# Half of the value projection in 512-column matmuls ahead of all scores, and later key projections begun before the scores of the pair ahead

## The chip, the cores and the metric

The kernel runs on one core of one Trainium2 chip. The core has a matrix engine (TensorE, PE in the profile; its weight loads are PEld), a vector engine (VectorE, DVE), a scalar engine (ScalarE, ACT), GpSimd (POOL), and SyncE (SP), whose queue issues all the DMAs of this kernel. Each engine works through its own instructions in order and waits for the others at semaphores. The metric is the device time of one execution in microseconds (us), as the median of a few runs. A profile is one more execution with the hardware profiler on; its span reaches from the first to the last instruction.

## The reference, cut to what matters

A decoder trunk for one sequence of 512 tokens with 1024 channels, all float32: a pooling layer with an MLP, then an attention layer with an MLP. The change lies in the attention layer. Keys and values come from one projection of the normed residual stream, queries from another, for 16 heads of 64 channels:

```
kv = jnp.matmul(rms_norm(x, kv_norm_g), w_kv).reshape(B, S, 2, N_HEADS, HEAD_DIM)
k = kv[:, :, 0].transpose(0, 2, 1, 3)
v = kv[:, :, 1].transpose(0, 2, 1, 3)
...
q = jnp.matmul(h, w_q[j]).reshape(B, S, N_HEADS, HEAD_DIM).transpose(0, 2, 1, 3)
o = stick_breaking_attention(q, k, v)
m = jnp.matmul(o.transpose(0, 2, 1, 3).reshape(B, S, HD), w_o[j])
```

Stick-breaking attention takes, for each query, the sigmoid of each score times the product of (1 - sigmoid) over all keys between that key and the query, and weighs the values with it; it is strictly causal. The kernel forms the products with a scan along the keys.

## The kernel before, in words

**Precision and matmuls.** Every float32 operand is split into a high part (a copy rounded to the matmul's type, on ScalarE) and a low part (the rest, a subtraction on VectorE). A product of two split operands is three matmuls: high x high, high x low, low x high (`mm3`, and `up_block` with the roles of the operands exchanged). A matmul streams up to 512 columns against a stationary 128x128 block into one bank of PSUM, of which there are eight; all of them go round under one tag, `ps`.

**Attention, by steps.** The 16 heads are eight pairs of two. The attention layer is written as a list of steps, `ATT_ORDER`, and TensorE runs them in exactly this order; the order of the other engines' instructions is left to the scheduler. A word of the list is a letter, an index and sometimes digits:

- `V` u, tiles: value projection for group u (four heads, 256 columns) and the named token tiles of 128. It is 24 matmuls of 256 columns per tile (8 channel blocks x 3), the normed tokens stationary and the weights moving, into half a bank; then ScalarE copies the high part and VectorE subtracts for the low part. Two weight tiles per group.
- `N` t: transposition of the normed token tile t of the layer's input (8 PE transposes, two copies, two subtractions). Tiles 2 and 3 are left over from the MLP before.
- `K` i: begins the key projection of pair i (`start`). `P` i: the rest of that key projection and the query projection of pair i (`project`, `queries_keys`), 24 matmuls of 512 columns each where nothing was begun, with the weights stationary and the tokens moving; then the splits `kh`, `kl`, `qh`, `ql`.
- `S` i: the scores of pair i (24 matmuls into six banks), and behind them the weights (`weights`): on ScalarE sigmoids of both signs (`against` writes `u`, `for_` writes `w`), on VectorE, head by head, a scan over 1280 entries (`scan`, tile `e`) and a product (`weigh`, tile `w`).
- `T` i: transposition of the weights of pair i, ten 128x128 transposes for its first head, then ten for its second, with copies `ah` and subtractions `al`. The first head's transposes wait for its `weigh`, the second head's for the other `weigh`.
- `A` i: products with the values (two banks), and the output pair `ohl` (`out_low`, `out`, `split`).
- `O` u, tiles: output projection of pairs 2u and 2u+1, added up in `y`. `E`: the end of the layer, in an order written out for all engines (`END_ORDER`).

**Before the change**, the list spreads the values over the layer: `V0` for tiles 0 and 1 covers the wait for `N2`, half of `K0` (its first 256 token columns) the wait for `N3`; `V1` stands in single tiles around the transposes of pairs 0 and 1.

**Weights.** All weights of the layer but two are scaled and split during the first MLP and put back into DRAM (`split_apart`, dictionary `kept`); they come back as two 512 KB DMAs each into one of four buffers (`w` three times, `wx` once), each DMA waiting for the last matmul on what the buffer held. `want` puts weights into a queue in the order of the list, `fill` and `make` issue the loads. The first two output weights (`("o", 0)`, `("o", 1)`) are not kept: they arrive raw and are split on ScalarE (line 170) and VectorE (line 172) during the attention layer. `behind` holds the last instructions of each engine, behind which later splits of weights may be issued.

Of the kernel before, what the change touches and what calls it, by code (L numbers as in the profile page):

```python
# [27 lines left out]
HD = 64  # L28
# [4 lines left out]
TS = [slice(t * P, (t + 1) * P) for t in range(T)]  # L33
NS = [slice(0, 512), slice(512, 1024)]
# [23 lines left out]

ATT_ORDER = [
    (w[0], int(w[1]), [int(c) for c in w[2:]])  # L60
    for w in """V001 N2 K0 N3 V02 P0 V03 S0 P1 V10 T0 V11 S1 A0 P2 T1 V12 A1 V13 S2 P3 T2 O00123 A2 S3 P4 V201 T3 S4
    A3 P5 V22 T4 V23 S5 A4 P6 V30 T5 V31 S6 A5 V323 P7 T6 E1""".split()
]


# [36 lines left out]
C_MIX_PRE0, C_KV, C_MIX_PRE1, C_MLP_PRE1 = range(4)  # L102
# [3 lines left out]
def trunk(ctx, tc, x, consts, grow, pw, wup, wdn, wq, wk, wv, wo, out):  # L106
    nc = tc.nc
# [22 lines left out]
    ident, gc = eye[:, :P], eye[:, P:]  # L130
# [23 lines left out]
    behind, latest = {}, {}  # L154
# [20 lines left out]
    def gains(lo, n):  # L175


        def scaled(raw):
            for k in range(n):
                c = raw[:, k * D // n : (k + 1) * D // n]  # L180
                nc.scalar.mul(c, c, gc[:, lo + k : lo + k + 1])  # L181
# [23 lines left out]
    apart, kept, going = [], {}, []  # L205
# [31 lines left out]
    def make():  # L237
        k, src, scaled = queue.pop(0)
        if k in kept:
            made[k] = place(k)  # L240
            for n, t in enumerate(made[k]):
                latest["sp"] = nc.sync.dma_start(t.bitcast(F32), kept[k][n])
            return
        made[k] = weight(src, place(k), scaled, dn_raw.pop(k, None))

    def fill(n=1):
        if gate[0]:
            behind.update(latest)
        for _ in range(n):
            if queue and len(made) < ahead and (queue[0][0][0] != "dn" or dn_pool[0]):  # L250
                make()

    def get(key):
        while key not in made:
            make()
        return made.pop(key)

    for l in range(2):
        if l == 1:
            n = len(queue)  # L260
            for what, i, part in ATT_ORDER:
                if what == "V" and 0 in part:
                    for h in range(2):
                        want(("v", i, h), wv[i, h], gains(C_KV * KC + 4 * h, 4))
                elif what == "P":
                    want(("k", i), wk[i], gains(C_KV * KC, KC))
                    want(("q", i), wq[i], gains(C_MIX_PRE1 * KC, KC))
                elif what == "O" and 0 in part or what == "E":
                    for c in range(2 * i, 2 * i + 2 if what == "O" else PAIRS):
                        want(("o", c), wo[c])  # L270
            apart.extend(x for x in queue[n:] if x[0] not in [("o", c) for c in range(2)])

            queue[n - GRP : n + GRP] = queue[n : n + GRP] + queue[n - GRP : n]
        for j in range(NJ):
            want(("up", l, j), wup[l, j])
        for j in range(NJ - GRP, NJ):
            want(("dn", l, j), wdn[l, j])
# [21 lines left out]
    def mm3(dst, ah, al, bh, bl, start, stop):  # L299
        nc.tensor.matmul(dst, ah, bh, start=start, stop=False)  # L300
# [193 lines left out]
    def y_tiles():  # L494
        return [work.tile([P, D], F32, tag=f"y{t}", name=name(f"y{t}")) for t in range(T)]
# [204 lines left out]
        fill(ahead)  # L700
        finish(l, squares[1:], w, y, lambda t, y: update(t, y, gpost))

    def up_block(pu, w, cols, last=False):
# [6 lines left out]
        for k in range(KC):  # L710
            nc.tensor.matmul(pu[:, cols], wh[:, k, :], xnh[:, k, cols], start=k == 0, stop=False)  # L711
            nc.tensor.matmul(pu[:, cols], wh[:, k, :], xnl[:, k, cols], start=False, stop=False)  # L712
            if not last:
                low(k)
        if last:
            for k in range(KC):
                low(k)


    with tc.tile_pool(name="mix0", bufs=1, reuse_waits="tile") as mp:  # L720
# [12 lines left out]
        at = P + 4 * KC  # L733
# [145 lines left out]
    with tc.tile_pool(name="att", bufs=1, reuse_waits="tile") as ap:  # L879
        att_pool[0] = ap  # L880

        def values(u, part):
            if u not in vs:
                w = [get(("v", u, h)) for h in range(2)]
                vs[u] = w, ap.tile([P, T, 4, 2, HD], F32R, tag="v", bufs=2, name=name("v"))
            w, v = vs[u]
            for s in part:
                need(s)
# [7 lines left out]
                pv4 = pv[:, :256].rearrange("p (h d) -> p h d", h=4)  # L896
                nc.scalar.copy(v[:, s, :, 0, :], pv4)
                nc.vector.tensor_tensor(
                    out=v[:, s, :, 1, :], in0=pv4, in1=v[:, s, :, 0, :].bitcast(F32), op=ALU.subtract
                )  # L900

        started = {}

        def start(key):

            need(0, 1)
            started[key] = ps(), get(key)
            up_block(*started[key], slice(0, S // 2))

        def project(key):  # L910
            need(*range(T))
            if key in started:
                pq, w = started.pop(key)
                up_block(pq, w, slice(S // 2, S))
            else:
                pq = ps()
                up_block(pq, get(key), slice(0, S))
            return pq
# [176 lines left out]
        vs, os, wos, y = {}, {}, {}, y_tiles()  # L1095
# [6 lines left out]
        def end():  # L1102

            p, last = PAIRS - 2, PAIRS - 1
            heads[last] = [Head(qk[last], last, a) for a in range(2)]
            w = {c: get(("o", c)) for c in range(2, 6)}
# [104 lines left out]
            with tc.manual_schedule(engines={on.PE, on.Activation, on.DVE, on.Pool, on.SP}):  # L1211
                for step, which in END_ORDER:
                    steps[step](*which)

        def until(key):
            while key not in made:
                make()
# [2 lines left out]

        def step(what, i, part):
            nonlocal gpost1
            if what == "V":
# [86 lines left out]
```

## Time and profile before

| what | value |
|---|---|
| time, median of 3 runs | 949.31 us (949.29 to 949.32) |
| time of the profiled execution | 949.25 us |
| its span | 947.4 us |
| TensorE busy | 938.1 us, 99% of the span, 4822 matmuls |
| VectorE, ScalarE, GpSimd busy | 73%, 59%, 4% |
| granted TensorE clock | 0.998 |
| DMA | 156.17 MB, mean 165 GB/s |

The profiled execution takes 1.85 us more than its span. Lines of a group view read: line of the kernel, engine, operation, output<-input, shape, count, busy time, mean duration. A line of the timeline reads: start (us), duration (us), engine, line, operation, tiles, shape, count, and in brackets how long the engine was idle before it and what ended that. A line of the table by windows reads: window, its length, then for each engine the busy time and the instructions that touch the window (those that reach across its edges included), the granted clock, the busy share of the DMA engines and GB/s. The attention layer lies at 368 to 592 us of the span.

### The profile page before, as it was taken

Reading aid. Unit: us, or ns where it says so; the run is one execution under the profiler, and the core shown is the slowest. Engines: PE = TensorE matmul, PEld = TensorE weight load, DVE = VectorE, ACT = ScalarE, POOL = GpSimd, SP = SyncE. Lnnn points to the kernel's source line nnn. Section 1 sums busy time; section 2 is a strip of 40 time slices with the busy share of each in tenths; the row PEclk is TensorE's granted clock in tenths of the full one; section 3 lists DMA queues with packets and bytes.
Section 4 is the critical chain, followed back from the end, with each engine's and each line's share of the span. In section 5 each row is a group of like instructions: output and inputs, shape, how many; then the busy total and the mean of one; then the engine's idle time right before and its main releaser. Section 6 shows DMA issues by size and latency. Waiting matters only on the chain.

```text
span 947.4 us, 12570 instructions
## 1 busy us (share of the span) xinstructions
PE 938.1 (99%) x4822; PEld 796.4 (84%) x4822; DVE 696.0 (73%) x797; ACT 559.1 (59%) x983; POOL 41.2 (4%) x83
## 2 busy tenths in 40 slices
PE   9999999999999999999999999999999999999996
PEld 7998888888888889888888988898888888888885
DVE  5875798988979876366466678874696966958756
ACT  6667979888775547345554444865545444444532
POOL 2300000000000004000000001200000000000002
PEclk9999999999999999999999999999999999999999
DMA  8254969789697760522425261442514233133102
GB/s 310 95 180 145 344 218 346 291 285 353 217 330 282 271 203 2 194 87 93 175 97 178 104 253 45 140 150 80 187 45 137 85 133 111 45 134 111 39 6 90
DMA packets 43263, 156.17 MB, mean 165 GB/s; under 512 B 4289, under 2 KB 4673, under 8 KB 43202
## 3 DMA queue, kind: packets, MB, share of 16 engines
q1 hardware_dynamic: 43202, 155.36, 46.4%
q8 instruction: 38, 0.62, 0.3%
q14 instruction: 23, 0.19, 0.1%
HBM read 121.79 MB, written 33.55 MB: 164 GB/s over the span
## 4 chain that ended last, share of the span: by engine, by line
PE 94%; DVE 1%; ACT 1%; POOL 1%; DMA 1%; issue 1%; SPq 0%; POOLq 0%; DVEq 0%; ACTq 0%
PE ps L589 28%; PE ps L711 15%; PE ps L708 15%; PE ps L712 15%; PE ps L300 4%; PE ps L302 4%; PE ps L301 4%; PE ps L1023 2%; PE ps L1048 2%; PE ps L1006 2%; PE ps L829 1%; PE ps L395 1%; ACT xn L285 1%; DMA band<-in_consts 1%; PE ps L801 1%; POOL stat L296 1%
## 5 line engine op out<-in xcount | busy, mean ns | idle before, releaser
L589 PE MATMUL ps<-w,a 128*128 128x512 f32 x1176 | 278.6, 389 | 0.0
L711 PE MATMUL ps<-xnh,w 128*128 128x512 f32 (+1 forms) x712 | 261.6, 369 | 0.0
L712 PE MATMUL ps<-xnl,w 128*128 128x512 f32 (+1 forms) x712 | 261.1, 368 | 0.0
L708 PE MATMUL ps<-xnh,w 128*128 128x512 f32 (+1 forms) x712 | 260.4, 368 | 0.1
L589 PEld LDWEIGHTS ps<-w,a 128*128 128x128 f32 x1176 | 220.7, 188 | 45.8 <-DVE w L282 0.2
L708 PEld LDWEIGHTS ps<-xnh,w 128*128 128x128 f32 x712 | 133.7, 189 | 22.5 <-DVE w L850 0.3
L712 PEld LDWEIGHTS ps<-xnl,w 128*128 128x128 f32 x712 | 134.2, 189 | 21.8
L711 PEld LDWEIGHTS ps<-xnh,w 128*128 128x128 f32 x712 | 133.9, 189 | 22.1
L598 DVE TENSOR_TENSOR y<-ps,y 128x512 f32<-128x512 f32 x124 | 84.2, 685 | 44.4 <-PE ps L589 44.2
L172 DVE TENSOR_TENSOR w<-raw,w 128x1024 fp32r<-128x1024 f32 x58 | 70.8, 1221 | 57.8 <-ACT w L170 57.7
L170 ACT CAST w<-raw 128x1024 fp32r<-128x1024 f32 x58 | 60.9, 1051 | 79.2 <-PE ps L708 79.1
L281 ACT CAST a<-r 128x768 fp32r<-128x768 f32 (+1 forms) x60 | 47.7, 794 | 72.2 <-PE ps L589 57.1
L987 DVE TENSOR_TENSOR_SCAN e<-u,begin 128x1280 f32<-128x1280 f32 x16 | 45.2, 2824 | 25.2 <-ACT u L971 24.9
L282 DVE TENSOR_TENSOR a<-r,a 128x768 fp32r<-128x768 f32 (+1 forms) x60 | 54.0, 899 | 12.3 <-ACT a L281 12.1
L281 ACT CAST w<-e 128x1536 fp32r<-128x1536 f32 (+1 forms) x30 | 41.9, 1395 | 23.4 <-DVE e L563 14.0
L282 DVE TENSOR_TENSOR w<-e,w 128x1536 fp32r<-128x1536 f32 (+1 forms) x30 | 49.4, 1646 | 2.0 <-ACT w L281 1.8
L181 ACT ACTIVATE apart<-apart,eye 128x128 f32<-128x128 f32 (+1 forms) x132 | 43.1, 408 | 0.8 <-DMA apart<-in_wk 0.8
L282 DVE TENSOR_TENSOR w<-w,w 128x1536 fp32r<-128x1536 f32 (+1 forms) x20 | 33.0, 1649 | 8.5 <-ACT w L281 8.1
L621 ACT ACTIVATE r<-ps 128x512 f32<-128x512 f32 x56 | 33.0, 590 | 8.9 <-PE ps L708 8.8
L282 DVE TENSOR_TENSOR w<-xn,w 128x1536 fp32r<-128x1536 f32 (+1 forms) x20 | 33.0, 1650 | 5.6 <-ACT w L281 5.5
L300 PE MATMUL ps<-w,xnh 128*128 128x256 f32 x128 | 36.7, 287 | 0.0
L622 ACT ACTIVATE r<-r 128x512 f32<-128x512 f32 x56 | 35.5, 633 | 1.3
(134 smaller groups left out, 1347.0 us busy)
## 6 DMA issues: line engine op xcount, KB each, us to landing
raw<-in_wup SPq DMA_DIRECT2D x64, 512.0 KB, 4.1
w<-kept SPq DMA_DIRECT2D x60, 512.0 KB, 4.2
kept<-wx SPq DMA_DIRECT2D x30, 512.0 KB, 4.8
w<-in_wdn SPq DMA_DIRECT2D x8, 1536.0 KB, 6.4
kept<-apart SPq DMA_DIRECT2D x24, 512.0 KB, 6.1
xn<-in_wdn SPq DMA_DIRECT2D x8, 1536.0 KB, 7.3
apart<-in_wk SPq DMA_DIRECT2D x7, 512.0 KB, 7.7
apart<-in_wq SPq DMA_DIRECT2D x7, 512.0 KB, 9.1
```

The lines of the kernel that those rows point to most:

```text
L170: nc.scalar.copy(hi, raw)
L172: nc.vector.tensor_tensor(out=lo, in0=raw, in1=hi.bitcast(F32), op=ALU.subtract)
L181: nc.scalar.mul(c, c, gc[:, lo + k : lo + k + 1])
L281: latest["act"] = nc.scalar.copy(hi, src)
L282: latest["dve"] = nc.vector.tensor_tensor(out=lo, in0=src, in1=hi.bitcast(F32), op=ALU.subtract)
L300: nc.tensor.matmul(dst, ah, bh, start=start, stop=False)
L589: nc.tensor.matmul(bank, a[:, x, q, TS[t]], w[:, z, q], start=start and q == 0 and k == 0, stop=q == self.n - 1 and k == 2, skip_group_che ...
L598: nc.vector.tensor_tensor(out=part, in0=bank, in1=part, op=ALU.add)
L708: nc.tensor.matmul(pu[:, cols], wl[:, k, :], xnh[:, k, cols], start=False, stop=k == KC - 1)
L711: nc.tensor.matmul(pu[:, cols], wh[:, k, :], xnh[:, k, cols], start=k == 0, stop=False)
L712: nc.tensor.matmul(pu[:, cols], wh[:, k, :], xnl[:, k, cols], start=False, stop=False)
L987: nc.vector.tensor_tensor_scan(out=self.e[:, ::-1], data0=self.u[:, 1:][:, ::-1], data1=begin[:, ::-1], initial=0.0, op0=ALU.mult, op1=ALU ...
```

## The change

- The values of groups 0 and 1 (heads 0 to 7) are projected together, 512 columns wide, ahead of all scores. The new step `H` i, tiles does half of the channels: `H0` blocks 0 to 3, `H1` blocks 4 to 7, each 12 matmuls of 512 columns per token tile, into a whole bank that is held between the two halves. After `H1` the bank is evacuated in two parts of 256 columns. Four weight tiles of two channel blocks each replace the two pairs of weight tiles, with the same number of bytes; the host packs them so.
- `start` takes all 512 token columns and the first three of the eight channel blocks (9 matmuls); `project` takes the other five (15) and the query projection (24). `K1` stands between `P0` and `S0`, `K2` between `T0` and `S1`, `K3` between `T1` and `S2`. `K0` and the single tiles of `V1` are gone.
- The output projection of the first two pairs is cut in two, around `T2`; `A2` follows `S3`; group 2 of the values has one tile before `T3` and one behind it.
- `values` and `project` no longer ask for the transposed tiles themselves (`N2` and `N3` stand in the list); `behind` is set once more after the end of the layer; two of the first weights are split and kept four places later in the first MLP, behind the queries of pair 1.

```
-    for w in """V001 N2 K0 N3 V02 P0 V03 S0 P1 V10 T0 V11 S1 A0 P2 T1 V12 A1 V13 S2 P3 T2 O00123 A2 S3 P4 V201 T3 S4
-    A3 P5 V22 T4 V23 S5 A4 P6 V30 T5 V31 S6 A5 V323 P7 T6 E1""".split()
+    for w in """H001 N2 H101 N3 H023 H123 P0 K1 S0 P1 T0 K2 S1 A0 P2 T1 K3 S2 A1 P3 O001 T2 O023 S3 A2 P4 V20 T3 V21
+    S4 A3 P5 V22 T4 V23 S5 A4 P6 V30 T5 V31 S6 A5 V323 P7 T6 E1""".split()
...
+                if what == "H" and not i and 0 in part:
+                    for h in range(4):
+                        want(("v", 0, h), wv[h], gains(C_KV * KC + 2 * h, 2))
...
+                elif what == "K":
+                    want(("k", i), wk[i], gains(C_KV * KC, KC))
...
+            at = [k for k, _, _ in apart].index(("v", 0, 2))
+            later = [apart.pop(at) for _ in range(2)]
+            at = [k for k, _, _ in apart].index(("q", 1)) + 1
+            apart[at:at] = later
...
+        def half_values(i, part):
...
+            for s in part:
+                if i == 0:
+                    half_bank[s] = ps()
+                for k in range(4 * i, 4 * i + 4):
+                    (wh, wl), c = half_w[k // 2], NS[k % 2]
+                    mm3(
+                        half_bank[s], xnh[:, k, TS[s]], xnl[:, k, TS[s]], wh[:, c], wl[:, c], k == 0, k == KC - 1
+                    )
+                if i == 1:
+                    for u in range(2):
+                        value_parts(vs[u][1], s, half_bank[s][:, u * 256 : u * 256 + 256])
+            if i == 1 and T - 1 in part:
+                fill(ahead)
...
         def start(key):
-            need(0, 1)
             started[key] = ps(), get(key)
-            up_block(*started[key], slice(0, S // 2))
+            up_block(*started[key], slice(0, S), ks=range(3))
 
         def project(key):
-            need(*range(T))
             if key in started:
                 pq, w = started.pop(key)
-                up_block(pq, w, slice(S // 2, S))
+                up_block(pq, w, slice(0, S), ks=range(3, KC))
...
+            behind.update(latest)
```

`value_parts` is the copy and the subtraction that stood at the end of `values`.

More of the change, by code (lines that the diff above doesn't have):

```diff
@@ L178, in scaled @@
         def scaled(raw):
-            for k in range(n):
-                c = raw[:, k * D // n : (k + 1) * D // n]
-                nc.scalar.mul(c, c, gc[:, lo + k : lo + k + 1])
+            m = max(n, 4)
+            for k in range(m):
+                c, at = raw[:, k * D // m : (k + 1) * D // m], lo + k * n // m
+                nc.scalar.mul(c, c, gc[:, at : at + 1])
         return scaled
@@ L261, in trunk @@
             for what, i, part in ATT_ORDER:
-                if what == "V" and 0 in part:
+                if what == "H" and not i and 0 in part:
+                    for h in range(4):
+                        want(("v", 0, h), wv[h], gains(C_KV * KC + 2 * h, 2))
+                elif what == "V" and 0 in part:
                     for h in range(2):
-                        want(("v", i, h), wv[i, h], gains(C_KV * KC + 4 * h, 4))
+                        want(("v", i, h), wv[2 * i + h], gains(C_KV * KC + 4 * h, 4))
+                elif what == "K":
+                    want(("k", i), wk[i], gains(C_KV * KC, KC))
                 elif what == "P":
-                    want(("k", i), wk[i], gains(C_KV * KC, KC))
+                    if ("k", i) not in [k for k, _, _ in queue]:
+                        want(("k", i), wk[i], gains(C_KV * KC, KC))
                     want(("q", i), wq[i], gains(C_MIX_PRE1 * KC, KC))
@@ L701, in mlp, with up_block @@
         finish(l, squares[1:], w, y, lambda t, y: update(t, y, gpost))
-    def up_block(pu, w, cols, last=False):
+    def up_block(pu, w, cols, last=False, ks=range(KC)):
         wh = w[0].rearrange("p (k c) -> p k c", k=KC)
@@ L708, in low @@
             nc.tensor.matmul(pu[:, cols], wl[:, k, :], xnh[:, k, cols], start=False, stop=k == KC - 1)
-        for k in range(KC):
+        for k in ks:
             nc.tensor.matmul(pu[:, cols], wh[:, k, :], xnh[:, k, cols], start=k == 0, stop=False)
@@ L880, in trunk, with value_tile, value_parts @@
         att_pool[0] = ap
+        def value_tile(u):
+            return ap.tile([P, T, 4, 2, HD], F32R, tag="v", bufs=2, name=name("v"))
+        def value_parts(v, s, src):
+            pv4 = src.rearrange("p (h d) -> p h d", h=4)
+            nc.scalar.copy(v[:, s, :, 0, :], pv4)
+            nc.vector.tensor_tensor(
+                out=v[:, s, :, 1, :], in0=pv4, in1=v[:, s, :, 0, :].bitcast(F32), op=ALU.subtract
+            )
+        half_w, half_bank = [], {}
+        def half_values(i, part):
+            if not half_w:
+                half_w.extend(get(("v", 0, h)) for h in range(4))
+                for u in range(2):
+                    vs[u] = None, value_tile(u)
+            for s in part:
[5 more added lines that the diff above has]
+                        half_bank[s], xnh[:, k, TS[s]], xnl[:, k, TS[s]], wh[:, c], wl[:, c], k == 0, k == KC - 1
+                    )
+                if i == 1:
+                    for u in range(2):
+                        value_parts(vs[u][1], s, half_bank[s][:, u * 256 : u * 256 + 256])
+            if i == 1 and T - 1 in part:
+                fill(ahead)
         def values(u, part):
             if u not in vs:
-                w = [get(("v", u, h)) for h in range(2)]
-                vs[u] = w, ap.tile([P, T, 4, 2, HD], F32R, tag="v", bufs=2, name=name("v"))
+                vs[u] = [get(("v", u, h)) for h in range(2)], value_tile(u)
             w, v = vs[u]
             for s in part:
-                need(s)
                 pv = ps()
@@ L895, in values @@
                     )
[L896 to L900, printed above, removed]
+                value_parts(v, s, pv[:, :256])
         started = {}
         def start(key):
-            need(0, 1)
             started[key] = ps(), get(key)
-            up_block(*started[key], slice(0, S // 2))
+            up_block(*started[key], slice(0, S), ks=range(3))
         def project(key):
-            need(*range(T))
             if key in started:
                 pq, w = started.pop(key)
-                up_block(pq, w, slice(S // 2, S))
+                up_block(pq, w, slice(0, S), ks=range(3, KC))
             else:
@@ L1222, in step @@
             nonlocal gpost1
-            if what == "V":
+            if what == "H":
+                half_values(i, part)
+            elif what == "V":
                 values(i, part)
@@ L1279 @@
     blocks = lambda w, n: w.reshape(KC, P, -1, n).transpose(2, 1, 0, 3)
-    wv = blocks(a["w_kv"][:, D:], 256).reshape(4, P, 2, D).transpose(0, 2, 1, 3)
+    wv = np.concatenate([
+        blocks(w, n).reshape(-1, P, c, D).transpose(0, 2, 1, 3).reshape(4, P, D)
+        for w, n, c in ((a["w_kv"][:, D : D + 512], 512, 4), (a["w_kv"][:, D + 512 :], 256, 2))
+    ])
     arrays = {
```

## The prediction

> **What bounds the kernel now.** I read the page's busy times first, then the list of waits for TensorE, then the timeline of the attention layer.
>
> ```profile
> span 947.4 us, 12570 instructions
> PE 938.1 (99%) x4822; PEld 796.4 (84%) x4822; DVE 696.0 (73%) x797; ACT 559.1 (59%) x983; POOL 41.2 (4%) x83
> ...
> PE ps L395 <- ACT xn L385: 0.5, 2, 0.3
> PE ps L801 <- DVE own L793: 0.2, 1, 0.2
> PE ps L1006 <- ACT ah L1012: 0.2, 1, 0.2
> ```
>
> TensorE sets the time: it hardly waits once it has begun, and in the attention layer only once for 0.15 us, before transposes of weights (line 1006). So an edit pays by taking matmul time away, and it costs whatever wait it opens on TensorE. The sum has these two sides.
>
> **Wide values.** The first table holds the seven stretches of `V0` and `V1` (192 matmuls of 256 columns), the second the two halves of `K0`, the query projection of pair 0 (24 matmuls of 512 columns), `O0` (48 of 512), then `T3` and `T0`.
>
> ```profile
> core 0: us, PE busy (x) PEld busy (x) DVE busy (x) ACT busy (x) POOL busy (x), PEclk, DMA share, GB/s
> 368.10:373.85 5.75, 5.75 (x50) 5.75 (x48) 4.74 (x8) 4.00 (x11) 2.12 (x4) 1.00 0.01 1
> ...
> 436.92:439.93 3.01, 3.01 (x26) 2.88 (x25) 1.59 (x3) 2.06 (x3) 0.00 (x0) 1.00 0.02 5
> sum 23.53, PE 23.53 PEld 23.13 DVE 15.06 ACT 10.56 POOL 2.12; mean PE 3.36 PEld 3.30 DVE 2.15 ACT 1.51 POOL 0.30
> ...
> 374.64:377.59 2.95, 2.95 (x28) 2.95 (x26) 1.53 (x3) 2.15 (x4) 2.70 (x16) 1.00 0.01 3
> 381.33:384.21 2.88, 2.88 (x27) 2.88 (x25) 0.42 (x1) 0.37 (x1) 0.00 (x0) 1.00 0.00 0
> 384.21:389.68 5.47, 5.47 (x27) 4.52 (x25) 0.69 (x1) 0.59 (x1) 0.00 (x0) 1.00 0.52 192
> 455.44:466.73 11.29, 11.29 (x51) 9.12 (x50) 3.61 (x7) 5.15 (x10) 0.00 (x0) 1.00 0.16 62
> 488.15:490.43 2.28, 2.28 (x22) 2.11 (x21) 1.39 (x3) 1.96 (x5) 0.00 (x0) 1.00 0.00 2
> 408.58:410.68 2.10, 2.10 (x22) 2.10 (x21) 1.27 (x3) 1.83 (x5) 0.00 (x0) 1.00 0.56 224
> ```
>
> The matmuls overlap, so I use pitch, not duration: 5.75/48 = 0.120 us for 256 columns; for 512 columns 5.47/24 = 0.228 in projections and 11.29/48 = 0.235 in `O0`. `H` has the form of `O0` (tokens stationary, 512 weight columns moving), so its 96 matmuls take 96 x 0.235 = 22.58 us where 23.53 stood: 0.95 us gained; at the other pitch 21.88, and 1.65. Half as many matmuls are almost no gain, because the pitch follows the columns. `K0` in two halves took 2.95 + 2.88 us, in one 5.47: 0.36 gained. Cutting `K1`, `K2`, `K3` at block 3 leaves their matmuls as they are.
>
> The Trainium skill, TensorE: Matmul & The Clock Gate, section Back-to-back issue gap, speaks against the idea too: it lists 262 cycles for 256 columns and 518 for 512, so two narrow matmuls cost 6 cycles more than a wide one. By that, an estimate at the 2.4 GHz the page names, the values gain 96 x 2.5 ns = 0.24 us and the sum below ends 0.7 us later. The rows have the larger difference, and I keep them.
>
> **Waits removed.** The wait before `T2` (0.15) goes, since `O001` now stands between `P3` and `T2`. `S4` no longer follows `T3` at once, so `T3` should take `T0`'s 2.10 instead of 2.28: 0.18. At the start of the second MLP the new `behind.update` moves the split of a down-projection weight behind the last normalization; it stands there between the squares of the last token tile:
>
> ```profile
> 613.20 1.03 ACT L170 CAST dn<-dn 128x1024 fp32r<-128x1024 f32 x1
> ```
>
> The longest line-395 wait above, 0.3 us, comes just behind it; I count 0.3 gained, at least 0. Gains: 0.95 + 0.36 + 0.15 + 0.18 + 0.3 = 1.94 us, between 1.31 and 2.64.
>
> **Waits added.** `T` needs the weights that ScalarE and VectorE make after `S`. What TensorE does between the two is the cover, and the change shortens it. TensorE first, then VectorE:
>
> ```profile
> 392.64 0.51 PE L1048 MATMUL ps<-kh,qh 64*128 64x512 f32 x2
> ...
> 393.96 0.29 PE L1048 MATMUL ps<-kh,qh 64*128 64x256 f32 x2
> ...
> 394.71 0.50 PE L711 MATMUL ps<-xnh,w 128*128 128x512 f32 x1
> ...
> 405.71 0.28 PE L300 MATMUL ps<-w,xnh 128*128 128x256 f32 x1
> ...
> 413.72 0.50 PE L1048 MATMUL ps<-kh,qh 64*128 64x512 f32 x2
> ...
> 415.77 0.50 PE L1023 MATMUL ps<-ah,v 128*128 128x512 f32 x1
> ...
> 418.37 0.45 PE L711 MATMUL ps<-xnh,w 128*128 128x512 f32 x1
> ...
> 439.93 0.50 PE L1048 MATMUL ps<-kh,qh 64*128 64x512 f32 x2
> ...
> 454.41 0.30 PE L1006 MATMUL ps<-eye,w 128*128 128x128 f32 x1 [0.15 <-ACT ah L1012]
> ```
>
> ```profile
> 404.97 0.67 DVE L932 TENSOR_TENSOR kl<-ps,kh 128x512 fp32r<-128x512 f32 x1
> 405.56 1.48 DVE L993 TENSOR_TENSOR w<-w,e 128x1280 f32<-128x1280 f32 x1
> ...
> 427.29 0.67 DVE L282 TENSOR_TENSOR ohl<-o,ohl 128x512 fp32r<-128x512 f32 x1
> 427.87 1.49 DVE L993 TENSOR_TENSOR w<-w,e 128x1280 f32<-128x1280 f32 x1
> ...
> 440.05 1.22 DVE L172 TENSOR_TENSOR w<-raw,w 128x1024 fp32r<-128x1024 f32 x1 [0.25 <-ACT w L170]
> ...
> 452.78 1.48 DVE L993 TENSOR_TENSOR w<-w,e 128x1280 f32<-128x1280 f32 x1
> 454.18 1.22 DVE L172 TENSOR_TENSOR w<-raw,w 128x1024 fp32r<-128x1024 f32 x1
> 455.31 0.68 DVE L932 TENSOR_TENSOR ql<-ps,qh 128x512 fp32r<-128x512 f32 x1
> 455.92 3.13 DVE L1016 TENSOR_TENSOR al<-ps,ah 128x512 fp32r<-128x512 f32 x6
> ```
>
> `T2`: its second half starts at 454.41, right behind the second product (452.78 + 1.48 = 454.26; the profile names ScalarE's `ah`, but in the program the transpose waits for the product). So 14.48 us pass from the start of `S2` to it, and the cover was just too short: scores, all 48 matmuls of `P3`, and the first half of `T2`. From `S0`, the second product ends after 407.04 - 392.64 = 14.40 us; with the same 0.15 of signalling, 14.55.
>
> `T0` after the change has this cover less nine matmuls: `K1` has run ahead of `S0`, `V10` is gone. TensorE arrives after 2.07 (scores) + 39 x 11.00/48 = 8.94 + 1.05 (half of `T0`) = 12.06 us. VectorE's chain keeps its instructions (scan, product, scan, product; the key split moves ahead of the second scan). Wait: 14.5 - 12.06 = 2.45 us, 2.4 to 2.5. Queued behind it are `K2` and `S1`, all later by as much.
>
> `T1` has `A0` in its cover too: 2.05 + 2.60 + 8.94 + 1.05 = 14.64 us. In its chain, the second scan is done 427.29 - 413.72 = 13.57 us after `S1`. In the changed program's order the splits of the two first output weights (line 172) move: before, one stood in idle time of VectorE (440.05), the other behind the second product (454.18). Now the first stands between the second scan and the second product of pair 1; its ScalarE copy needs the buffer of `k2`, free long before. So 13.57 + 1.13 (454.18 to 455.31) + 0.59 (key split, 404.97 to 405.56) + 1.49 + 0.15 = 16.93, and a wait of 2.29 us. Without the weight split 1.16, the lower bound.
>
> `S2`: its banks come from `T1`'s six subtractions, before which the split of `ohl` (0.58, 427.29 to 427.87), `ql` (0.61) and now the second weight split (1.13) stand. The fifth, which the last score bank needs, ends at 16.78 + 0.58 + 0.61 + 1.13 + 3.13 x 5/6 + 0.15 = 21.86 after `S1`; TensorE is there after 16.93 + 1.05 + 2.06 (`K3`) + 1.32 (393.96 less 392.64) = 21.36: 0.5 us, between 0 and 0.8. `T3` has `A2`, all of `P4` and `V20` ahead of it, 3 us more than its chain needs.
>
> Costs: 2.45 + 2.29 + 0.5 = 5.24 us, between 3.56 and 5.7.
>
> **Costed at nothing.** `N2`, `N3`: the normalized tiles are there at 370.97 and 376.79,
>
> ```profile
> 369.65 1.32 ACT L385 ACTIVATE xn<-x,stat 128x512 f32<-128x512 f32 x2
> ...
> 375.44 1.35 ACT L385 ACTIVATE xn<-x,stat 128x512 f32<-128x512 f32 x2
> ```
>
> and TensorE comes at 368.10 + 24 x 0.235 = 373.74, then, after 0.79 of `N2` (373.85 to 374.64) and `H101`, at 380.2. Without that cover the loss would be what of 2.8 and 8.7 us stayed open. Loads: `v` tiles fill all four buffers, so `k0` (two DMAs on SP's queue, `q0`'s two behind them) is issued only when `H023` leaves its first buffer, 30 matmuls or 7.0 us before its first use.
>
> ```profile
> DMA to landing us min/median/max: 2.6/4.3/10.4
> ```
>
> The median lands in time. `K1` (2.05 us) covers the split of `q0` before `S0`. The same number of instructions goes over ScalarE and VectorE, and the evacuations of `H` are off the path since `A0` comes 30 us later.
>
> **Sum.** The profiled execution took 949.25, 0.06 below the median: 949.31 - 1.94 + 5.24 = 952.6 us. With the favourable ends 949.31 - 2.64 + 3.56 = 950.2, with the others 949.31 - 1.31 + 5.7 = 953.7.
>
> **Rivals.** (1) The weight splits fall out of pair 1's chain because ScalarE or VectorE reaches them elsewhere: `T1` waits 1.16, `S2` not at all: 950.97, within 0.2%. For it: both stood in idle time before; against: engines keep their order. (2) Not slower: the covers hold. The place is the second half of `T0`; it decides if the second product is there within 12.06 us of `S0`, 2.4 earlier than in any pair above. Then only the gains are left, 947.4. Against it stands `T2`, which waited with more cover. (3) `k0` lands late: with the longest landing, 10.4 - 7.0 = 3.4 us more, 956.0. For it: all `v` buffers are held; against: the median. (4) The clock: after the last matmul TensorE's clock falls.
>
> ```profile
> 940.00:941.00 1.00, 0.26 (x3) 0.05 (x1) 0.71 (x2) 0.25 (x1) 0.36 (x1) 1.00 0.20 76
> 943.00:944.00 1.00, 0.00 (x0) 0.00 (x0) 1.00 (x3) 0.00 (x0) 0.00 (x0) 1.00 0.00 0
> 944.00:945.00 1.00, 0.00 (x0) 0.00 (x0) 0.04 (x1) 0.00 (x0) 0.00 (x0) 0.50 0.89 322
> ```
>
> It stayed at 1.00 through 3.7 us of idling and was 0.50 after. If a wait of 2.4 us were enough, and the clock took 3.7 us to come back, each of the two waits would cost half of that more: 956.3. The Trainium skill, same page, section What's actually happening, puts the drop after an idle window of about 3.4 us, which agrees with this row and speaks against the rival.
>
> **How the numbers follow.** Forecast 0.74 (950.2 to 953.7 is its own range), rival 1 0.12, 2 0.06, 3 0.04, 4 0.04. About 0.2%, 1.9 us, can be told from no change here, so slower means above 951.2: most of the forecast and rivals 3 and 4, 0.80; same 0.15; faster, a part of rival 2, 0.05. The range reaches a little beyond the forecast's own ends, 949.9 to 954.6.
>
> **What would show it.** TensorE waits of some 2.3 us inside `T0` and `T1`, each before the second ten transposes and released by VectorE's product, a smaller one inside `S2`, none before `T2`; `H` at 0.235 us a matmul; a line-172 split between scan and product of pair 1. TensorE without waits there, or a wait on a DMA at the first key matmul, would prove me wrong.

## The result, and the profile after

| what | before | after |
|---|---|---|
| time, median (executions) | 949.32 us (948.75 to 949.79; 10) | 952.08 us (951.04 to 955.06; 10) |
| ratio, 95% interval | | 1.0033 [1.0023, 1.0042] |
| profiled execution, its span | 949.25, 947.4 us | 952.13, 950.4 us |
| TensorE busy | 938.1 us | 936.5 us |

The change makes the kernel 0.3% slower, 0.5 us less than predicted and inside the predicted range. The page and the list of TensorE's waits of the changed kernel:

```profile
span 950.4 us, 12326 instructions
...
PE 936.5 (99%) x4702; PEld 789.3 (83%) x4702; DVE 695.2 (73%) x797; ACT 559.2 (59%) x983; POOL 41.3 (4%) x83
...
PE ps L1042 <- DVE w L1029: 4.3, 2, 2.3
...
PE ps L406 <- ACT xn L396: 0.2, 1, 0.2
```

TensorE has 1.6 us less to do and 3.0 us more to live through. Two waits, 4.3 us together, are new, both at the transposes of attention weights (line 1042), both for VectorE's product (line 1029). The 0.2 us before `T2` and one of the two waits for `xn` are gone. Where the waits lie, in TensorE's timeline of the changed kernel (pair 0, then pair 1):

```profile
415.90 1.25 PE L1042 MATMUL ps<-eye,w 128*128 128x128 f32 x10
419.44 1.28 PE L1042 MATMUL ps<-eye,w 128*128 128x128 f32 x10 [2.28 <-DVE w L1029]
420.48 0.48 PE L722 MATMUL ps<-xnh,w 128*128 128x512 f32 x1
...
436.32 1.25 PE L1042 MATMUL ps<-eye,w 128*128 128x128 f32 x10
439.64 1.28 PE L1042 MATMUL ps<-eye,w 128*128 128x128 f32 x10 [2.07 <-DVE w L1029]
440.68 0.48 PE L722 MATMUL ps<-xnh,w 128*128 128x512 f32 x1
```

The first head's ten transposes run at once, the second head's ten wait. `T0` takes 420.48 - 415.90 = 4.58 us and `T1` 440.68 - 436.32 = 4.36, where each took 2.10 before. VectorE in the same stretches has no gap ahead of the second product:

```profile
414.95 2.82 DVE L1023 TENSOR_TENSOR_SCAN e<-u,begin 128x1280 f32<-128x1280 f32 x1
417.80 1.49 DVE L1029 TENSOR_TENSOR w<-w,e 128x1280 f32<-128x1280 f32 x1
...
433.56 2.82 DVE L1023 TENSOR_TENSOR_SCAN e<-u,begin 128x1280 f32<-128x1280 f32 x1
436.30 1.20 DVE L172 TENSOR_TENSOR w<-raw,w 128x1024 fp32r<-128x1024 f32 x1
437.42 0.68 DVE L968 TENSOR_TENSOR kl<-ps,kh 128x512 fp32r<-128x512 f32 x1
438.02 1.48 DVE L1029 TENSOR_TENSOR w<-w,e 128x1280 f32<-128x1280 f32 x1
```

417.80 + 1.49 = 419.29, and 0.15 us later the second half of `T0` starts. For pair 1, the weight split of line 172 stands between scan and product.

The gains, in the table by windows of the changed kernel: the three stretches of `H`, the nine matmuls of `K2`, and, at the start of the second MLP, the up-projection block and the last eight transposes; below them the same two windows of the kernel before.

```profile
core 0: us, PE busy (x) PEld busy (x) DVE busy (x) ACT busy (x) POOL busy (x), PEclk, DMA share, GB/s
368.31:373.76 5.45, 5.45 (x26) 4.46 (x24) 4.41 (x7) 3.64 (x10) 2.12 (x4) 1.00 0.00 2
374.55:380.09 5.54, 5.54 (x27) 4.54 (x26) 2.14 (x4) 2.90 (x6) 2.68 (x16) 1.00 0.00 1
380.88:391.86 10.98, 10.98 (x52) 9.10 (x50) 2.71 (x6) 1.94 (x5) 0.00 (x0) 1.00 0.50 167
...
420.48:422.73 2.25, 2.25 (x14) 1.59 (x12) 2.25 (x6) 0.97 (x3) 0.00 (x0) 1.00 0.00 0
...
617.23:620.18 2.95, 2.95 (x27) 2.95 (x25) 2.33 (x7) 2.88 (x9) 0.55 (x1) 1.00 0.45 122
620.18:620.98 0.80, 0.80 (x11) 0.80 (x9) 0.74 (x1) 0.80 (x5) 0.00 (x0) 1.00 0.99 410
```

```profile
613.64:617.05 3.41, 3.11 (x27) 2.91 (x26) 3.12 (x8) 3.01 (x9) 0.55 (x1) 1.00 0.58 181
617.05:618.08 1.03, 1.03 (x9) 0.84 (x9) 1.03 (x1) 1.03 (x4) 0.00 (x0) 1.00 1.04 426
```

`H` takes 5.45 + 5.54 + 10.98 = 21.97 us for 96 matmuls, 0.229 each, 1.56 us less than the 23.53 before. The start of the second MLP takes 3.75 us instead of 4.44. `K2`'s nine matmuls take 2.25 us; at the pitch of an unbroken projection they would take 2.05.

### The profile page after: what moved, and what is told of

It reads as the page before. It is cut to its first block, busy times and chain, and to the rows that moved or that the text cites. A ratio compares the mean times of both kernels' runs of the same rounds, so it can differ in the third digit from the quotient of the medians.

```text
span 950.4 us, 12326 instructions
## 1 busy us (share of the span) xinstructions
PE 936.5 (99%) x4702; PEld 789.3 (83%) x4702; DVE 695.2 (73%) x797; ACT 559.2 (59%) x983; POOL 41.3 (4%) x83
## 4 chain that ended last, share of the span: by engine, by line
PE 94%; DVE 2%; ACT 1%; DMA 1%; POOL 1%; issue 0%; SPq 0%; POOLq 0%; DVEq 0%; ACTq 0%
PE ps L600 28%; PE ps L722 15%; PE ps L719 15%; PE ps L723 15%; PE ps L311 4%; PE ps L313 4%; PE ps L312 4%; PE ps L1059 2%; PE ps L1042 2%; PE ps L1084 2%; PE ps L840 1%; PE ps L406 1%; DMA band<-in_consts 1%; PE ps L812 1%; DVE e L1023 1%; ACT xn L296 1%
## 5 line engine op out<-in xcount | busy, mean ns | idle before, releaser
L719 PEld LDWEIGHTS ps<-xnh,w 128*128 128x128 f32 x704 | 132.2, 188 | 23.0 <-DVE w L861 0.3
L722 PEld LDWEIGHTS ps<-xnh,w 128*128 128x128 f32 x704 | 132.3, 188 | 22.3
L296 ACT ACTIVATE xn<-y 128x512 f32<-128x512 f32 (+1 forms) x25 | 15.3, 613 | 32.1 <-DVE y L478 28.5
```

## The experiments

Each run changes the changed kernel unless it says otherwise; it was timed next to executions of the kernel before on the same chip, whose medians lie between 949.30 and 949.49 us. TensorE's granted clock fell for a few microseconds in some executions (section 4 shows how), and their times hold that too, so the profiles of the parts decide. The profiles of runs 1, 3, 4 and 9 have such falls in the attention layer, the others none.

### 1. `K1` whole again

```
-P0 K1 S0 P1 T0
+P0 S0 P1 T0
```

> K1 stays whole: the nine matmuls of the key projection of pair 1 go back from ahead of S0 to between S0 and T0. Theory (a wait is the length of VectorE's chain less the matmul time between scores and transposes): the cover of T0 grows by 2.05 us, from 12.06 to 14.1 against a chain of 14.5, so T0's wait falls from 2.28 us to about 0.4; the split of q0 loses its cover, and a new wait of 0.7 to 1.5 us opens before or inside S0. T1's wait stays 2.1. Net 0.4 to 1.2 us less than the changed kernel's 952.08: about 951.3. Rival (T0's wait is set by something that moves with it, not by the cover): T0 keeps 2.3 us, and S0's new wait comes on top: about 953.2.

951.67 us (950.53 to 952.32, 9 executions). TensorE's timeline shows `S0` waiting, and `T0` as one group of twenty transposes with no wait in it:

```profile
403.77 0.50 PE L1084 MATMUL ps<-kh,qh 64*128 64x512 f32 x2 [0.68 <-ACT qh L967]
...
417.10 2.38 PE L1042 MATMUL ps<-eye,w 128*128 128x128 f32 x20
419.23 0.48 PE L722 MATMUL ps<-xnh,w 128*128 128x512 f32 x1
```

`T0` takes 2.13 us, so its wait is gone altogether; `S0` is dearer by the 0.68 shown and a quarter of a microsecond inside it (2.33 us instead of 2.06). The wait at `T0` was missing cover, and the nine matmuls were most of what it missed. The 0.4 us that the sum left did not show, because the chain became shorter too: the key split of pair 1, ahead of the second scan in the changed kernel (414.35), comes behind the second product here (418.03), and from the start of the first scan to the end of the second product VectorE takes 8.94 us (409.17 to 418.11) instead of 9.28 (410.01 to 419.29).

`T1` waits 2.07 us as before, and behind that wait the granted clock of the profiled execution is 0.50 from 438.39 to 441.81. The nine times stand in two groups: four at 950.5 to 950.8 us with mean clocks of 0.998 and 0.999, and five at 951.7 to 952.3, the profiled one among them, with 0.996 and 0.997. Section 4 takes this up.

### 2. The first two output weights split behind `T1`

```
+            if hold[0] and queue and queue[0][0] in (("o", 0), ("o", 1)):
+                return
...
                 transposed(heads[i])
                 behind.update(latest)
+                if i == 1:
+                    hold[0] = False
+                    fill(2)
```

> The splits of the first two output weights are begun only behind T1 (their loads too). Theory (the line-172 split sits in pair 1's chain): the second product of pair 1 comes 1.12 us earlier, less 0.58 because the split of ohl moves up into the place that comes free: T1's wait falls from 2.07 us to about 1.5, S2's 0.08 goes, T0's 2.28 stays; 0.5 to 0.7 us less than the changed kernel, about 951.5. Rival (rival 1 of the prediction turned round: these splits only fill idle time of VectorE, the scan or the loads set the time): T1 keeps 2.07 us, and the time stays at 952.1, or is later if O001 now waits for its weights.

951.20 us (950.70 to 953.36, 11 executions). VectorE's timeline of pair 1 from the end of the second scan, and below it the second half of `T1` in TensorE's:

```profile
435.78 0.67 DVE L971 TENSOR_TENSOR kl<-ps,kh 128x512 fp32r<-128x512 f32 x1
436.36 0.68 DVE L296 TENSOR_TENSOR ohl<-o,ohl 128x512 fp32r<-128x512 f32 x1
436.96 1.49 DVE L1032 TENSOR_TENSOR w<-w,e 128x1280 f32<-128x1280 f32 x1
```

```profile
438.60 1.28 PE L1045 MATMUL ps<-eye,w 128*128 128x128 f32 x10 [1.52 <-DVE w L1032]
```

The weight split is out of the chain, the split of `ohl` has taken its place, and the wait is 1.52 us, down from 2.07, where 1.5 was expected. What stands between scan and product is paid in full.

### 3. The values in 256 columns, in the same places

```
-H001 N2 H101 N3 H023 H123 P0
+V001 N2 V101 N3 V023 V123 P0
```

> The half of the values that stands ahead of all scores is made in matmuls of 256 columns again, in the same places and as one unbroken block (192 matmuls for 96), with the weights laid out as before. Theory (the pitch has a fixed part, 0.120 to 0.1226 us for 256 columns against 0.229 for 512): the block grows from 21.97 us to between 23.0 and 23.5, so the time grows by 1.0 to 1.6 us, to about 953.4. Rival (the pitch follows the columns, 6 cycles more for two narrow matmuls than for a wide one, and the slow pitch of the kernel before came from its seven short stretches): 0.2 us more, about 952.3.

955.09 us (953.71 to 956.54, 5 executions). The block in windows:

```profile
367.83:373.58 5.75, 5.75 (x50) 5.75 (x48) 4.74 (x8) 4.00 (x11) 2.12 (x4) 1.00 0.01 1
374.37:380.20 5.83, 5.83 (x52) 5.83 (x50) 1.95 (x4) 2.52 (x5) 2.69 (x16) 1.00 0.02 4
380.99:392.58 11.59, 11.59 (x100) 11.59 (x98) 2.80 (x6) 2.04 (x5) 0.00 (x0) 1.00 0.50 177
```

5.75 + 5.83 + 11.59 = 23.17 us against 21.97: the width is worth 1.20 us, inside what the rows had promised, and the other 0.36 of the 1.56 came from joining seven short stretches into three. The cycles that the Trainium skill lists for a matmul by itself (TensorE: Matmul & The Clock Gate, section Back-to-back issue gap) give 0.24 for the width, an estimate; the measurement decides against it here. Most of the rest of this run's extra time is the clock (below): its profiled execution shows two falls that the changed kernel's does not, and its one execution with a mean clock of 0.999 took 953.71 us.

### 4. Without the line behind the layer's end

```
-            behind.update(latest)
```

> Only the line that puts the work on weights behind the last normalization of the attention layer is taken out again. Theory (the split of a down-projection weight returns ahead of the last token tile's normalization): the wait of 0.3 us at the last 10 transposes of the second MLP's start comes back, and the up-projection block ahead of it takes 3.41 us again where it takes 2.96: 0.3 to 0.7 us more than the changed kernel, about 952.6. Rival (those 0.7 us came from the attention layer's new order): the start of the second MLP stays as it is, 952.1.

954.56 us (953.77 to 955.61, 5 executions). ScalarE's timeline has the split of the down-projection weight back between the squares, and the list of TensorE's waits has the wait back:

```profile
619.56 1.03 ACT L170 CAST dn<-dn 128x1024 fp32r<-128x1024 f32 x1
```

```profile
PE ps L406 <- ACT xn L396: 0.5, 2, 0.3
```

The up-projection block takes 3.40 us and the eight transposes 1.03 again, 0.68 more than with the line. That is the theory's number. The other 1.8 us of this run were expected by neither side; its profile shows where they are. `K2`'s nine matmuls, 2.25 us in the changed kernel, take 3.82 (420.20 to 424.03), with nothing waited for. The clock column says why:

```profile
420.00:421.00 1.00, 1.00 (x8) 0.86 (x6) 1.00 (x3) 1.00 (x3) 0.00 (x0) 0.77 0.07 16
421.00:422.00 1.00, 1.00 (x4) 0.81 (x3) 1.00 (x3) 0.18 (x1) 0.00 (x0) 0.50 0.00 0
422.00:423.00 1.00, 1.00 (x3) 0.77 (x3) 0.67 (x2) 0.00 (x0) 0.00 (x0) 0.50 0.00 0
423.00:424.00 1.00, 1.00 (x3) 0.33 (x1) 0.00 (x0) 0.00 (x0) 0.00 (x0) 0.52 0.00 0
424.00:425.00 1.00, 1.00 (x10) 0.85 (x10) 0.00 (x0) 0.00 (x0) 0.00 (x0) 1.00 0.00 0
...
441.00:442.00 1.00, 1.00 (x6) 1.00 (x7) 1.00 (x3) 0.00 (x0) 0.00 (x0) 0.51 0.00 0
```

Behind the wait of `T0` the granted clock falls to a half at 420.54 (0.54 of that microsecond at 1.00 and the rest at 0.50 make 0.77) and is back at 423.95. It falls again behind `T1`'s wait, at 441.02. Each fall costs some 1.6 us (3.82 - 2.25 at `K2`; 0.92 in the transposes and 0.70 in `K3` behind `T1`). The profile of the changed kernel has the same two waits and 1.00 throughout. That was a rival of the prediction, and it needed runs of its own.

### 5. Useless work in the two waits

```
             elif what == "T":
+                if i < 2:
+                    spare = ps()
+                    for k in range(9):
+                        nc.tensor.matmul(spare, xnh[:, 0, TS[0]], xnh[:, 0, :], start=k == 0, stop=k == 8)
                 transposed(heads[i])
```

> Nine more matmuls of 512 columns, whose result nobody reads, stand ahead of T0 and nine ahead of T1: 18 x 0.228 = 4.1 us of added work for TensorE. Theory (T0 and T1 wait for VectorE's chain, 2.28 and 2.07 us, and the clock falls in those executions in which such a wait fills more than about half of one of the clock's windows of 3.41 us): the waits shrink to about 0 and the added work costs 0.2 to 0.5 us (two restarts), no execution loses 1.6 us to the clock, so the times lie close together, 951.5 to 952.8, none above 953.2. Rival (TensorE's own work sets the time, and the scatter of the changed kernel has another source): 4.1 us more, about 956, with executions spread over 4 us as the changed kernel's.

951.82 us (951.69 to 952.18, 9 executions). Of the 4.3 us in the list of waits this is left:

```profile
PE ps L1042 <- DVE w L1029: 0.2, 1, 0.2
```

18 matmuls, 4.1 us of TensorE's time, cost nothing that the times show. And the executions lie within 0.5 us of each other where the changed kernel's lie 4 us apart: with the waits filled, the profiled execution has no fall of the clock, and no other shows one in its time.

### 6. All splits behind the second product

To run 2 is added:

```
+                with late(p - 1, what == "k" and p < 3):
                     latest["dve"] = nc.vector.tensor_tensor(out=lo, in0=src, in1=hi.bitcast(F32), op=ALU.subtract)
...
+            with late(p + 1, p < 1):
                 split(o, *os[p])
```

`late(p, at)` queues, where `at` is true, VectorE's part of its block behind the second product of pair p.

> As in the run that begins the first two output weights behind T1; in addition the key splits of pairs 1 and 2 and the split of ohl of pair 0 are queued behind the second product of VectorE. Theory: T0's chain loses the key split (0.59 us), so its wait falls from 2.28 to 1.7 us; T1's chain loses the weight split and the key split (1.12 + 0.59 us), so its wait falls from 2.07 to about 0.4. Both are then too short for the clock to fall often. About 2.3 us less than the changed kernel's undisturbed executions (951.9): 949.6. Rival (the scans, not the splits between them, or the splits' later place behind the products, which S1 and S2 need, set the time): T0 keeps 2.3 us, or S1 and S2 wait as much as T0 and T1 gain: 951.2.

949.89 us (949.51 to 950.55, 11 executions), 2.2 us below the changed kernel and 0.4 above the kernel before, from which it can't be told apart (ratio 1.0006 [0.9997, 1.0015]). The list of waits:

```profile
PE ps L1046 <- DVE w L1033: 2.3, 2, 1.8
```

1.79 us at `T0` and 0.48 at `T1`, where 1.7 and 0.4 were expected; `S1` and `S2` wait for nothing. So the splits behind the second product delay nothing there; what is left of the wait belongs to the scans and products themselves.

### 7. The cover given back

To run 6 is added: `K2` and `K3` begin in two steps (the digits are the channel blocks), and `O001` takes pair 0 for all four banks before pair 1.

```
-P0 K1 S0 P1 T0 K2 S1 A0 P2 T1 K3 S2 A1 P3 O001 T2
+P0 K1012 S0 P1 K2012 T0 K2345 S1 A0 P2 K30123 T1 K345 S2 A1 P3 O001 T2
```

> As the run with all splits queued behind the products; in addition K2 is begun in two steps (blocks 0 to 2 ahead of T0, 3 to 5 behind it), K3 too (blocks 0 to 3 ahead of T1, 4 and 5 behind it), and O001 takes all products with pair 0 first. Theory (only cover was missing, and O001 gives it back at T2): no wait of more than 0.3 us is left in the attention layer; against the changed kernel's undisturbed 951.9 that is 4.4 us of waits less 0.4 us of restarts: about 948.0, and below the kernel before (949.4), with times close together. Rival (the cover taken from P3 is missing at O001, which needs ohl of pair 1): a new wait of 1 to 4 us stands there, 949 to 952.

947.72 us (947.33 to 948.35, 11 executions) against 949.49 (31 executions of the kernel before): ratio 0.9982 [0.9973, 0.9991]. It beats both kernels. The waits above 0.3 us in its list, and `T0` and the first matmul of `O001` in the timeline:

```profile
PE ps L770 <- POOL warm L736: 1.3, 1, 1.3
PE ps L815 <- DVE own L807: 0.6, 1, 0.6
```

```profile
418.00 2.37 PE L1050 MATMUL ps<-eye,w 128*128 128x128 f32 x20
420.13 0.48 PE L725 MATMUL ps<-xnh,w 128*128 128x512 f32 x1
...
452.49 0.40 PE L314 MATMUL ps<-w,ohl 128*128 128x512 f32 x1
```

The two waits on top belong to the first layer. `T0` takes 2.13 us, `O001` starts right behind `P3`; the rival's wait there did not come. `T1` (2.36 us) and `S2` (2.39) are still 0.2 to 0.3 us longer than without waits. So the idea of the change was sound; what it lacked was cover at `T0` and `T1`, taken by key projections that run ahead in too large a step, and chains free of splits.

### 8. The one line alone, in the kernel before

```
                 for step, which in END_ORDER:
                     steps[step](*which)
+            behind.update(latest)
```

> The kernel before with the one line alone that queues the work on weights behind the last normalization of the attention layer. Theory: the second MLP's start loses its wait of 0.3 us and its longer block (3.41 to 2.96 us), nothing else moves: 0.7 us less than the kernel before, about 948.7. Rival (the split only moves to another place where TensorE waits for it): within 0.2 us of the kernel before.

948.72 us (948.37 to 949.10, 11 executions) against 949.49, ratio 0.9992 [0.9984, 1.0001]. The interval just holds 1; the profile has the block at 2.96 us, the eight transposes at 0.79 and no wait between them, so the 0.7 us are real. The rest of the change costs by so much more.

### 9. A longer wait

In run 6, `K1` begins with six blocks instead of three.

```
-P0 K1 S0 P1 T0 K2
+P0 K1012345 S0 P1 T0 K2012
```

> As the run with all splits queued behind the products, but K1 begins with six of its eight blocks ahead of S0 instead of three, which takes nine more matmuls (2.05 us) out of T0's cover. Theory of the cover: T0's wait grows from 1.8 to 3.8 us, and everything behind it is 2.05 us later: 949.9 + 2.05 = 951.9. Theory of the clock (it falls to 0.5 for one window of 3.41 us when a window of 3.41 us is idle for more than some 1.8 of it): a wait of 3.8 us, however it lies, puts more than that into at least one window, so now every execution loses, by how much of the low clock falls on matmuls: up to 1.7 us more for one window. No execution below 952.1, the median near 953.2, the mean clock 0.996 or 0.997 instead of 0.998. Rival (the slow matmuls behind the waits have another cause than the length of the wait): 951.4 to 952.4 in all executions, the clock at 1.00.

953.82 us (953.25 to 954.70, 5 executions), every one slower than the 951.9 that the cover alone would make, mean clock 0.994 to 0.997. Clock in windows, of its profile:

```profile
419.00:420.00 1.00, 0.00 (x0) 0.00 (x0) 0.90 (x2) 0.00 (x0) 0.00 (x0) 0.89 0.97 381
420.00:421.00 1.00, 0.00 (x0) 0.00 (x0) 1.00 (x2) 0.00 (x0) 0.00 (x0) 0.50 0.14 49
...
426.00:427.00 1.00, 1.00 (x5) 0.51 (x4) 0.00 (x0) 0.00 (x0) 0.00 (x0) 0.70 0.00 0
```

`T0` waits 0.47 and 3.15 us. The clock falls at 419.78, in the middle of the wait, and stays low for 6.8 us, two windows; the second ten transposes take 2.05 us instead of 1.04 and `K2`'s nine matmuls 3.87 instead of 2.25. By their times and clocks all five executions had a fall; that is inferred for the four that have no profile. A wait makes the clock fall, and this longer one seems to have done it each time.

### 10. The changed kernel once more

> The changed kernel itself once more, to see how its times and its mean clock go together. Theory of the clock: two waits of 2.3 and 2.1 us, each of which is followed by a fallen clock or not, depending on how the windows lie; so its times stand in steps about 1.6 us apart, near 951.9 (no fall), 953.5 (one) and 955.1 (two), and the mean clock of an execution is lower by 0.002 for each fall. Rival (scatter of another source): times spread evenly, with no relation to the clock.

952.42 us (951.30 to 953.87, 5 executions). The two longest, 953.24 and 953.87, have mean clocks of 0.996 and 0.997, the others 0.998 and 0.999. Of the ten executions of the result, 953.88 and 955.06 have 0.997 and 0.995, the other eight (951.04 to 952.36) 0.998 and 0.999. Time and clock go together. The mean clock alone is not enough: run 8's profile has 0.997 with no fall before the end of its matmuls. Clean steps as in run 1 do not show here, since the executions taken as undisturbed differ by 1.4 us themselves, and why these do is open. Open too is why all executions of run 4 and most of run 3 lost time to the clock, and only 4 of 15 of the changed kernel, with waits as long.

## Why the prediction was right, step by step

Right in sign and mechanism: two waits, 2.28 and 2.07 us in the trace, at the second ten transposes of `T0` and `T1`, released by VectorE's product. By its terms, with the sizes from the two profiles:

| step | predicted, us | measured, us |
|---|---|---|
| `T0`'s wait | +2.45 | +2.48 (4.58 less 2.10) |
| `T1`'s wait, with the weight split in its chain | +2.29 | +2.26 (4.36 less 2.10) |
| `S2` | +0.5 | +0.45 (442.93 to 445.45, less 2.07) |
| restarts | not in the sum | +0.65 |
| wide values | -0.95 | -1.56 |
| `K0` in one piece | -0.36 | -0.35 |
| `T2`'s wait | -0.15 | -0.34 |
| `T3`, `S4` | -0.18 | -0.25 |
| start of the second MLP | -0.3 | -0.69 |
| sum | +3.30 | +2.65 |

The profiled executions differ by 952.13 - 949.25 = 2.88 us; 0.21 of the remaining 0.23 lies ahead of the attention layer, which begins at 368.31 instead of 368.10.

- **Covers and chains.** 14.5 us of chain against 12.06 of cover held (404.87 to 419.44 is 14.57, and the first half of `T0` ends after 12.08), and runs 1, 5 and 7 show it from three sides. The weight split in pair 1's chain held as well; rival 1 fell, as the timeline shows line 172 where it was forecast. Run 2 shows its price: taking it out saves 0.55 us of wait, its 1.12 less the 0.58 of the `ohl` split that moves up.
- **The upper end.** 5.7 us of costs is not the sum of the ends named, 2.5 + 2.29 + 0.8 = 5.59; the upper end lies 0.1 us too high.
- **Where luck helped.** The gains came out at 3.19 us instead of 1.94, and 0.65 us of restarts had no term. The two errors partly cancel, so the time lies nearer to the forecast than the terms do. Nor does the median execution hold a fall of the clock: with falls, executions of the changed kernel reached 955.06 us, outside the range.
- **Wide values, mis-sized.** "`H` has the form of `O0`", and so its pitch of 0.235, was the wrong row: `H` runs at 0.229, the pitch of the projections. Of the 1.56, joining the stretches was worth 0.36 us (run 3), which the prediction had not named apart from the width.
- **The second MLP, mis-sized.** The prediction counted the wait alone, 0.3. The matmuls ahead of it shrank too, from 3.11 to 2.95, and the transposes behind it from 1.03 to 0.80; what a short wait does to the work around it had no term. Runs 4 and 8 give 0.7 for the line.
- **Restarts, left out.** A block of nine matmuls behind transposes takes 0.2 us more than nine in a stream (`K2`, `K3`), the output projection and group 2 of the values in two parts 0.09 and 0.16 more. "Cutting `K1`, `K2`, `K3` at block 3 leaves their matmuls as they are" was true of their number only.
- **Costed at nothing.** `N2`, `N3`, the loads and the evacuations of `H` cost nothing indeed: TensorE's list has no wait on a DMA, so rival 3 fell, and its only wait for `xn`, 0.2 us, lies behind the layer's end (596.00).
- **Rival 4, the clock, was waved away too soon.** Its price (half of 3.7 us for each wait) was near the measured 1.6, but it was taken to happen always or never, and one row spoke for never. That row was a matter of phase: the clock fell at 944.00, 3.75 us behind the last matmul's end, and the window of 3.41 us ahead of the fall began at 940.59, after that end. In runs 6 and 8 the same fall came 2.1 and 2.2 us behind the last matmul's end (940.51 and 939.86). It happens in some executions: 4 of the 15 of the changed kernel by their times and mean clocks. The median hardly shows it, the scatter does. The Trainium skill (TensorE: Matmul & The Clock Gate, section What's actually happening) has a free-running window of 3413 ns, which the falls here agree with; the prediction read from its idle window of about 3.4 us that a wait must last so long, and runs 4 and 9 show that it need not.

## What to carry to other kernels

When work is moved ahead, subtract it from the place it leaves: there it was the cover of a chain on another engine, and the chain's length (scan, product and every split the scheduler may slip between them) less the matmul time left is the new wait, to a tenth of a microsecond here wherever the order in the chain was the one assumed (in run 1 it was not). A shortage of cover can be handed on in steps, a little from each stage, until a stage with surplus work pays it, and what is not needed by the chain can be queued behind it. Judge a stall of two microseconds by more than its length: it can halve TensorE's clock behind itself, and a time that scatters where it did not before is a sign of it.

## What the runs showed of the hardware

**Windows of the clock.** The two falls of run 4 lie 441.02 - 420.54 = 20.48 us apart. In run 3 the waits lie a microsecond later, and the falls are at 421.46 and 441.94, again 20.48 apart:

```profile
421.00:422.00 1.00, 1.00 (x7) 0.83 (x6) 1.00 (x3) 1.00 (x3) 0.00 (x0) 0.73 0.00 0
...
441.00:442.00 1.00, 0.04 (x1) 0.07 (x2) 1.00 (x2) 0.71 (x2) 0.00 (x0) 0.97 0.00 0
```

That is six times 3.413 us, and each low stretch is one such length (420.54 to 423.95). The other stretches of run 4's clock are whole multiples as well: 416.43 us from its first rise at 4.11 to the first fall is 122 of them, 505.17 from the last return at 444.43 to the fall behind the work is 148. So the clock is set at the ends of windows that run on whatever the kernel does. In the windows ahead of these four falls, and of those of runs 1 and 9, TensorE idled 2.0 to 2.1 of the 3.41 us: in run 4, of the window from 417.13 to 420.54, until the transposes began at 419.17. In the changed kernel the clock falls last behind the end of the work:

```profile
946.00:947.00 1.00, 0.00 (x0) 0.00 (x0) 0.93 (x3) 0.00 (x0) 0.00 (x0) 0.94 0.01 2
947.00:948.00 1.00, 0.00 (x0) 0.00 (x0) 0.00 (x0) 0.00 (x0) 0.00 (x0) 0.50 0.99 356
```

155 windows ahead of that fall, at 946.87, one begins at 417.81. It holds 1.63 us of `T0`'s wait (to 419.44), and at its end the clock did not fall. So the bound lies between 1.6 and 2.0 us of idling in 3.41, and the phase of the windows decides for a wait of 2.3 us. In run 9 the second window, 419.78 to 423.19, was idle to 421.04 only, 1.26 us, yet the clock was not given back at its end: to get it back took a busier window than to keep it. The starts of runs 6, 8 and 9 agree. The first matmul comes at 1.30 us in all three, and the first matmuls, of 512 columns, stand 0.43 us apart until the clock rises and 0.22 after. In run 6 the rise comes at 3.94, at the end of a window with 0.8 us of idling; in runs 8 and 9 a window with 1.3 to 1.4 us of idling ends near 3.4 without a rise, which comes one window later, at 6.8.

**Width and weight loads.** In run 3 the column PEld is as full as the window (11.59 of 11.59) at 23.17/192 = 0.121 us a matmul; in `H` it is 9.10 of 10.98. That fits a pitch set by the weight loads at 256 columns and by the columns at 512; it was not tried by itself.
